# The first expert's tokens by one-hot products, the tables between its weight tiles, and the branch for excess tokens at the end

## The chip, the cores and the metric

The kernel runs on one core of one Trainium2 chip. Its engines are TensorE (PE), VectorE (DVE), ScalarE (ACT), GpSimd (POOL) and SyncE (SP); they run side by side and wait for each other by semaphores. SP, ACT and POOL also issue DMAs. The metric is the device time of one execution in microseconds (us). The kernel before takes 1837.77 us, the median of three runs (1836.67 to 1837.92).

## The reference

Two blocks work on 512 tokens of 1024 features, in float32. The first ends in a mixture of 32 experts, of which each token uses four:

```python
h      = rms_norm(x, norm_moe_w)
logits = h @ router_w + router_b              # (512, 32)
gates  = softmax(top_4(logits))               # 4 experts for each token
for e in range(32):                           # gate_up (1024, 2048), down (1024, 1024)
    g, u = split_even_odd(h_e @ gate_up[e] + b_gate_up[e])
    g, u = minimum(g, 7), clip(u, -7, 7)
    y += gate_e * (((u + 1) * g * sigmoid(1.702 * g)) @ down[e] + b_down[e])
```

This is condensed from the reference's words. After the experts come an embedding of the token (`p`, `ple_proj_w`, `ple_gate_w`) and a norm, and then the second block: a sparse attention by an indexer, a chunked causal attention, and the product with `w_out_2`.

## The kernel before

The program has three stages: `front` (norm, retention, pooling, `w_out`, router), `moe`, and `back` (embedding and attention). What moves lies in `moe` and on its two edges.

**The router's row tiles.** The 512 tokens are four row tiles of 128. `front` computes h tile by tile; the router takes each tile's top four, writes the normalised rows to `hn_d` in HBM (L667, L668) and a copy of h to `y_d` (L619), to which the experts' outputs are later added. For each token and expert, `by_e` holds the token's place among the expert's tokens and its gate.

**Experts, tiles and chunks.** An expert's weights are 12 chunks of 1 MiB, each holding two tiles of 128 rows by 1024 columns, so 384 chunks in all. Float32 precision comes from three products of rounded parts: ACT copies a tile to a rounded high part (L937), DVE subtracts that from the tile for the low part (L938), and PE multiplies. The experts are taken in the order of their load. For "many" experts (0 and the odd ones up to 29; up to 96 tokens) a tile costs six matmuls of 512 columns, in the helper `mm3`: high by x's high part (L187), high by x's low part (L188), low by x's high part (L189), first for one half of the columns and then for the other. "Few" experts (the even ones from 2 on, and 31; up to 64 tokens) have both parts of x side by side and four matmuls for a tile (L942). The bias product (L1051) stands ahead of a half's eight tiles.

**The streams and the jobs.** Two generators, `many` and `few`, yield after each tile; from the 24th tile on (`ALONE`) they take turns. Between tiles, `next_tile` runs jobs that are due: tables of tokens (`table`), an expert's gather by indirect DMA (L890) and its transposes (L905) in `fetch`, the activation (`clamped`, `folded`), and the scaled output that POOL adds to `y_d` by indirect DMA (`out`, L1028). Their place in the program, on every in-order engine, is thus fixed by the count of tiles. The two PSUM banks of the jobs are lent out by `bank`.

**The ring.** Weight chunks arrive in 7 slots: two of the pool `wr`, three of `wr2`, and two halves of the tile h, which is free once h has been copied out. An eighth early chunk goes to `ys`, the buffer of outputs. SP issues the loads in order (L167; L1167 for the early ones); each waits until its slot's tiles have been split.

**The start of the experts.** In a row and ahead of the first tile stand: the gates and the table of expert 0, its gather, the split of the gate-up biases (`bt`, L1162), `arrange` (ranks the experts by load, writes their order, `beyond` and, by L799 to L805, all tables' input), the early loads, `overflow`, and the transposes of expert 0's gathered tokens. `overflow` is a branch, `tc.If(most > 0)` at L1080: were an expert to hold more tokens than its tile, the rest would be worked there. Its condition is the number `beyond`, computed from the data; here it is zero, so the branch isn't taken. On the untaken side each engine waits for its own work, SP for all loads that it and ACT have issued, POOL for all of its own DMAs, and POOL then counts those up on SP's behalf.

**The end.** `gated_bias` adds the gates times the experts' down biases; it starts at expert 11. After the last tile `back` loads p (`pt`, L1215), `ple_proj_w` (`wp`, L1217) and the sums (`h<-y_d`, L1265), multiplies `pt` by `wp`, and sums squares of h (L251).

Of the kernel before, what the change touches and what calls it, by code (L numbers as in the profile page):

```python
# [19 lines left out]
D = 1024  # L20
NE = 32
# [14 lines left out]
ALONE, LAG = 24, 5  # L36
# [106 lines left out]
class Kern:  # L143
# [189 lines left out]
    def run(self):  # L333
        tc, nc, I = self.tc, self.nc, self.I
        with ExitStack() as g:
# [8 lines left out]
            with ExitStack() as a:  # L344
                wr2 = a.enter_context(tc.tile_pool(name="wr2", bufs=3))
                self.wr = [wr2, wr, wr2, wr, wr2]
                self.wh = [wh] * 2
                self.rp = a.enter_context(tc.tile_pool(name="rp", bufs=1))
                self.junk = self.rp.tile([128, D], BF16, name="junk")
                with ExitStack() as f:  # L350
                    self.front(f)
                with ExitStack() as f:
                    Q = f.enter_context(tc.tile_pool(name="mq", bufs=2, reuse_waits="tile"))
                    self.wr = [wr, wr2, wr, wr2, wr2] + [Part(self.h[:, 2 * i:2 * i + 2, :]) for i in range(2)]
                    self.moe(f, Q)
                self.wr, self.wh = [wr], [wh]
# [303 lines left out]
    def router(self, t, hT, s2, hg, T):  # L660
# [99 lines left out]
    def arrange(self, P, T, sel):  # L760

        nc, c = self.nc, self.c
        cp = self.tr.tile([128, 512], F32, tag="tr", name="tr")
# [6 lines left out]
        nc.vector.scalar_tensor_tensor(out=key, in0=cp[:, 0:NE], scalar=float(NE), in1=c["key"], op0=ALU.mult, op1=ALU.add)  # L770
        nc.vector.tensor_tensor(out=own, in0=key, in1=c["sel"], op=ALU.mult)
# [10 lines left out]
        kp = self.tr.tile([128, 512], F32, tag="tr", name="tr")  # L782
        nc.tensor.matmul(kp[:, 0:NE], rank[0:NE, 0:1].to_broadcast([NE, 128]), perm[0:NE, 0:NE], start=True, stop=True)
        ki = P.tile([128, NE], I32, name="ki")
        nc.vector.tensor_copy(ki, kp[:, 0:NE])
        self.order = P.tile([128, NE], I32, name="order")
# [10 lines left out]
        tp = self.tr.tile([128, 512], F32, tag="tr", name="tr")  # L797
        for t in range(NT):
            nc.tensor.transpose(tp[0:64, self.tok(t)], self.by_e[:, t].rearrange("p a e -> p (a e)"), c["ident"])  # L799
        bt = T.tile([128, S], F32, tag="ag", name="by_t")[0:64]  # L800
        nc.scalar.activation(bt, tp[0:64, :], AF.Copy)
        bp = self.tr.tile([128, NT, 2, NE], F32, tag="tr", name="tr")
        for t in range(NT):
            nc.tensor.matmul(bp[:, t].rearrange("p a e -> p (a e)"), bt[:, self.tok(t)], perm, start=True, stop=True)
        nc.vector.tensor_copy(self.by_i, bp)  # L805
        self.gates(self.by_i[:, :, 1], self.tcols, NE, T)

    def moe(self, f, Q):
# [18 lines left out]
        xgs = [P.tile([CAP, D], F32, name=f"xg{i}") for i in range(2)]  # L827
# [44 lines left out]

        def tables(e, t3):
            for j in range(BATCHES[e]):
                tabs[e + j] = [a[:, j:j + 1] for a in t3]

        def table(e):

            ps, free = yield from bank()
# [44 lines left out]
        def chunks(src, ps, pair, raw=(), bias=None, few=False):  # L924


            if bias is not None and not few:
                for n in range(2):
                    bias(n, True)
            for c0 in range(0, 8, 2):  # L930
                w = raw.pop(0) if raw else self.load(src(c0 * 128, 256).rearrange("o (k p) n -> p (o k) n", p=128), 2, 1024)
                for kk in range(2):
                    k = c0 + kk
                    hi, lo = self.next(parts)
                    if raw:
                        nc.vector.tensor_copy(hi[:, 0:1], tabs[0][1])
# [180 lines left out]
        def gated_bias():  # L1117

            bd = T.tile([128, D], F32, tag="yb", name="bd", bufs=1)
            for r in range(0, 128, NE):  # L1120
                nc.sync.dma_start(bd[r:r + NE], I["expert_b_down"][0])
            bs = P.tile([128, D], F32R, name="bs")
            yield 8
            nc.scalar.activation(bs, bd, AF.Copy)
            nc.vector.tensor_tensor(out=bs[64:128], in0=bd[64:128], in1=bs[64:128].bitcast(F32), op=ALU.subtract)
            rows = P.tile([128, NT], I32, name="rows")
            for t in range(NT):
                g4 = T.tile([128, 4, NE], F32, tag="g4", name="g4", bufs=1)
                nc.vector.tensor_copy(g4, self.G[:, t, None, :].to_broadcast([128, 4, NE]))
                nc.vector.tensor_scalar(rows[:, t:t + 1], c["far"], 128.0 * t - FAR - 1, None, op0=ALU.add)  # L1130
                yield 1
                tp, free = yield from bank()
                nc.tensor.transpose(tp[:, 0:128], g4.rearrange("p a e -> p (a e)"), c["ident"])
                yield LAG
                gT = T.tile([128, 128], F32R, tag="gT", name="gT", bufs=1)
                nc.scalar.activation(gT, tp[:, 0:128], AF.Copy)
                yield 1
                for r in (32, 96):
                    q = slice(r, r + NE)
                    nc.vector.tensor_tensor(out=gT[q], in0=tp[q, 0:128], in1=gT[q].bitcast(F32), op=ALU.subtract)  # L1140
                free()
                yield 1
                y = T.tile([128, D], F32, tag="yb", name="yb", bufs=1)
                for n in range(2):
                    ps, free = yield from bank()
                    nc.tensor.matmul(ps, gT, bs[:, n * 512:n * 512 + 512], start=True, stop=True)
                    yield LAG
# [4 lines left out]
                yield 8  # L1152
# [5 lines left out]
        nc.vector.tensor_copy(bt[:, 0:1], tabs[0][1])  # L1158
        nc.scalar.activation(bt, braw, AF.Copy)
        for r in (32, 96):  # L1160
            q = slice(r, r + NE)
            nc.vector.tensor_tensor(out=bt[q], in0=braw[q], in1=bt[q].bitcast(F32), op=ALU.subtract)  # L1162
        self.arrange(P, T, sel)
# [6 lines left out]
        raws = [early(i, self.next(self.wr).tile([128, 2, 1024], F32, tag="wr", name="wr")) for i in range(7)]  # L1170
        overflow()
        raws.append(early(7, ys))

        def stream(es):

            for e, after in zip(es, es[1:] + [None]):
# [5 lines left out]
                if e == 11:  # L1182
                    job(gated_bias())
# [19 lines left out]
        while self.jobs:  # L1203
            next_tile()

# [478 lines left out]
```

## Time and profile before

| | |
|---|---|
| median of 3 runs | 1837.77 us |
| profiled execution | 1836.86 us |
| its span | 1835.0 us |
| mean granted TensorE clock | 0.981 |
| PE busy | 1739.8 us (95%) |
| PE weight loads busy | 1285.0 us (70%) |
| DVE busy | 1529.2 us (83%) |
| ACT busy | 1193.9 us (65%) |
| POOL busy | 221.2 us (12%) |
| HBM read | 470.90 MB |

The rows are read from the one profiled execution, whose times run from the start of its span; what lies around the span is 1836.86 - 1835.0 = 1.86 us. Busy shares are means over stages that differ: the router's last tile ends near 222 us, the experts' weights stream until about 1363 us, and the rest is `back`. A releaser behind an arrow is the event that ended an idle time last. A tile's name without a number stands for all of its buffers.

### The profile page before, as it was taken

The numbers are of one execution on the slowest core, as the hardware profiler recorded it, in microseconds if no ns is written. First come the engines' busy times: TensorE is split into PE (matmuls) and PEld (weight loads), VectorE is DVE, ScalarE is ACT, GpSimd is POOL, SyncE is SP. The second block draws the span as 40 slices with busy tenths as digits, with TensorE's granted clock in tenths as the row PEclk, the third lists the DMA queues.
The fourth block names the chain that finished last, engine by engine and source line by source line (L and its number), as shares of the span: only waits on it lengthen the run. The fifth ranks groups of instructions, "written<-read, shape, count | busy, mean of one in ns | idle before, by whom it ended". The sixth has DMA issues, their size and how long they took to land. (4 is left out here: it accounts for less than half of the span.)

```text
span 1835.0 us, 24671 instructions
## 1 busy us (share of the span) xinstructions
PE 1739.8 (95%) x8375; PEld 1285.0 (70%) x8379; DVE 1529.2 (83%) x2665; ACT 1193.9 (65%) x1591; POOL 221.2 (12%) x124
## 2 busy tenths in 40 slices
PE   8999779999999998999999999999978999999999
PEld 6887657666776775766666666766656777787776
DVE  5574589999999998999999999999977769999542
ACT  5224258778878777887788788788875445554431
POOL 0011212131111311210201211110310000000000
PEclk9999879999999998999999999999999999999999
DMA  8224469999999999999999999999985222201211
GB/s 283 85 95 149 147 219 354 384 354 389 378 391 386 373 379 363 341 391 383 379 374 393 384 371 395 383 382 391 391 291 188 91 63 82 89 28 53 84 54 40
DMA packets 148295, 493.18 MB, mean 269 GB/s; under 512 B 14369, under 2 KB 18721, under 8 KB 148160
## 3 DMA queue, kind: packets, MB, share of 16 engines
q1 hardware_dynamic: 137600, 462.02, 67.1%
q0 software_dynamic: 8640, 24.78, 6.0%
q10 hardware_dynamic: 1920, 4.72, 0.7%
q8 instruction: 68, 1.11, 0.2%
q14 instruction: 67, 0.55, 0.1%
HBM read 470.90 MB, written 25.17 MB: 270 GB/s over the span
## 5 line engine op out<-in xcount | busy, mean ns | idle before, releaser
L938 DVE TENSOR_TENSOR wl<-wr,wh 128x1024 fp32r<-128x1024 f32 x550 | 641.8, 1215 | 30.9 <-ACT wh L937 30.1
L937 ACT ACTIVATE wh<-wr 128x1024 fp32r<-128x1024 f32 x550 | 544.1, 1050 | 46.3 <-DMA wr<-in_expert_w_gate_up_dram 19.0
L938 DVE TENSOR_TENSOR wl<-h,wh 128x1024 fp32r<-128x1024 f32 x216 | 252.9, 1215 | 13.8 <-ACT wh L937 13.8
L189 PE MATMUL mm<-wl,x 128*96 128x512 f32 x512 | 208.6, 407 | 16.9 <-DVE wl L938 15.9
L937 ACT ACTIVATE wh<-h 128x1024 fp32r<-128x1024 f32 x216 | 214.9, 1050 | 14.6 <-DMA h<-in_expert_w_gate_up_dram 7.3
L187 PE MATMUL mm<-wh,x 128*96 128x512 f32 x512 | 206.0, 402 | 0.7 <-ACT x L239 0.4
L188 PE MATMUL mm<-wh,x 128*96 128x512 f32 x512 | 203.2, 397 | 0.0
L1028 POOL DMA_INDIRECT y_d<-ys,gi x48 | 116.9, 2435 | 640.5 <-ACT ys L1026 390.8
L942 PE MATMUL mm<-wl,x 128*128 128x512 f32 x512 | 169.8, 412 | 1.4 <-DVE wl L938 1.2
L942 PE MATMUL mm<-wh,x 128*128 128x512 f32 x512 | 168.1, 399 | 3.1 <-ACT wh L937 3.1
L189 PEld LDWEIGHTS mm<-wl,x 128*96 128x96 f32 x512 | 82.9, 162 | 72.5 <-DVE wl L938 41.1
L189 PE MATMUL mm<-wl,a 128*96 128x512 f32 x256 | 103.9, 406 | 15.1 <-DVE wl L938 15.0
L942 PEld LDWEIGHTS mm<-wh,x 128*128 128x128 f32 x512 | 96.2, 189 | 31.2 <-ACT wh L937 4.0
L187 PE MATMUL mm<-wh,x2h 128*128 128x512 f32 (+2 forms) x288 | 114.6, 398 | 0.3 <-ACT x2h L239 0.3
L188 PE MATMUL mm<-wh,x2l 128*128 128x512 f32 (+2 forms) x288 | 111.3, 387 | 0.0
L189 PE MATMUL mm<-wl,x2h 128*128 128x512 f32 (+2 forms) x288 | 111.0, 387 | 0.1
L942 PEld LDWEIGHTS mm<-wl,x 128*128 128x128 f32 x512 | 89.0, 189 | 29.7 <-DVE wl L938 13.2
L181 DVE TENSOR_TENSOR wl<-wr,wh 128x2048 fp32r<-128x2048 f32 (+3 forms) x40 | 76.6, 1915 | 36.7 <-ACT wh L180 36.5
L188 PEld LDWEIGHTS mm<-wh,x 128*96 128x96 f32 x512 | 83.6, 163 | 33.3 <-DVE x L241 0.4
L187 PEld LDWEIGHTS mm<-wh,x 128*96 128x96 f32 x512 | 83.2, 163 | 31.3 <-ACT wh L937 3.5
L890 POOL DMA_INDIRECT xg<-hn_d,gi x32 | 67.6, 2114 | 291.4 <-PE tr L905 229.5
L187 PE MATMUL mm<-wh,a 128*96 128x512 f32 x256 | 102.2, 399 | 0.0
(437 smaller groups left out, 3271.2 us busy)
## 6 DMA issues: line engine op xcount, KB each, us to landing
wr<-in_expert_w_gate_up_dram SPq DMA_DIRECT2D x184, 1024.0 KB, 12.6
wr<-in_expert_w_down_dram SPq DMA_DIRECT2D x91, 1024.0 KB, 13.0
h<-in_expert_w_gate_up_dram SPq DMA_DIRECT2D x71, 1024.0 KB, 11.9
h<-in_expert_w_down_dram SPq DMA_DIRECT2D x37, 1024.0 KB, 13.5
wr<-in_w_in_dram SPq DMA_DIRECT2D x20, 1024.0 KB, 5.1
wr<-in_w_out_dram SPq DMA_DIRECT2D x8, 1024.0 KB, 4.9
wr<-in_ple_gate_w_dram SPq DMA_DIRECT2D x4, 1024.0 KB, 5.3
wr<-in_w_in_dram SPq DMA_DIRECT2D x4, 512.0 KB, 5.6
```

What stands on the lines that cost most here:

```text
L181: nc.vector.tensor_tensor(out=lo[:, sl], in0=raw[:, sl], in1=hi[:, sl].bitcast(F32), op=ALU.subtract)
L187: mm(out, a[0], b[0], start=first, stop=False)
L188: mm(out, a[1], b[0], start=False, stop=False)
L189: mm(out, a[0], b[1], start=False, stop=last)
L890: nc.gpsimd.indirect_dma_start(out=xgs[LESS[e]][0:m], out_offset=None, in_=self.hn_d[:, :], in_offset=bass.IndirectOffsetOnAxis(ap=tabs[e] ...
L937: nc.scalar.activation(hi, w[:, kk], AF.Copy)
L938: nc.vector.tensor_tensor(out=lo, in0=w[:, kk], in1=hi.bitcast(F32), op=ALU.subtract)
L942: nc.tensor.matmul(ps[:, n, :], pair[2][:, k, :], part[:, n * 512:n * 512 + 512], start=k == 0 and part is hi, stop=k == 7 and part is lo)
L1028: nc.gpsimd.indirect_dma_start(out=self.y_d[:, :], out_offset=bass.IndirectOffsetOnAxis(ap=rows[0:m // n], axis=0), in_=y[o:o + m // n], i ...
```

## The change

Line numbers have grown in the changed file: L938 becomes L952, L942 L956, L905 L922, L1051 L1068, L1028 L1045, L1080 L1097, L1215 L1251.

1. Expert 0's tokens are no longer gathered. Four comparisons build `first`, a one-hot matrix of tokens by places, from `by_e`; 32 float32 matmuls (L1182) multiply the rows of h by it, straight into the transposed form that L922 would give. For that the router writes the normalised rows over h in SBUF, and `hn_d` is copied from there. The two loads into h's halves come after these matmuls.
2. The bias split, the gates, the tables of the next experts and `arrange` become one job, `startup`, whose pieces stand between the first tiles.
3. For many experts a tile's matmuls run in another order: both halves of the columns by high and high, both by high and low, then both of the low part. The bias product moves to the eighth tile.
4. The ring gets an eighth slot (pool `wr4`); the ninth early chunk goes to `ys`.
5. `overflow` moves behind the last tile, and `gated_bias` to expert 29, the last of the many. Its buffers change.
6. `ALONE` goes from 24 to 32.

```diff
-ALONE, LAG = 24, 5
+ALONE, LAG = 32, 5
...
-                    self.wr = [wr, wr2, wr, wr2, wr2] + [Part(self.h[:, 2 * i:2 * i + 2, :]) for i in range(2)]
+                    more = f.enter_context(tc.tile_pool(name="wr4", bufs=1, reuse_waits="tile"))
+                    self.wr = [wr, wr2, wr, wr2, wr2, more] + [Part(self.h[:, 2 * i:2 * i + 2, :]) for i in range(2)]
...
-            nc.scalar.activation(hg[j], hg[j], AF.Copy, scale=rs)
-            nc.scalar.dma_start(self.hn_d[self.tok(t), 512 * j:512 * j + 512], hg[j])
+            o = slice(512 * j, 512 * j + 512)
+            nc.scalar.activation(self.h[:, t, o], hg[j], AF.Copy, scale=rs)
+            nc.scalar.dma_start(self.hn_d[self.tok(t), o], self.h[:, t, o])
...
-            if bias is not None and not few:
-                for n in range(2):
-                    bias(n, True)
...
-                        nc.vector.tensor_copy(hi[:, 0:1], tabs[0][1])
+                        nc.vector.tensor_copy(hi[:, 0:1], first[:, NT - 1, 0:1])
...
-                        for n in range(2):
-                            nn = slice(n * 512, n * 512 + 512)
-                            self.mm3(ps[:, n, :], (pair[0][:, k, :], pair[1][:, k, :]), (hi[:, nn], lo[:, nn]),
-                                     bias is None and k == 0, k == 7)
+                        if bias is not None and k == 7:
+                            for n in range(2):
+                                bias(n, False)
+                        for x, part in ((pair[0], hi), (pair[1], hi), (pair[0], lo)):
+                            for n in range(2):
+                                nc.tensor.matmul(ps[:, n, :], x[:, k, :], part[:, n * 512:n * 512 + 512],
+                                                 start=k == 0 and x is pair[0] and part is hi, stop=k == 7 and part is lo)
...
-        self.gates(self.G[:, :, 0:2], self.tcols0, 2, T)
-        tables(0, self.slots(0, BATCHES[0], Q))
-        gather(0)
...
-        self.arrange(P, T, sel)
+        first = P.tile([128, NT, CAP], F32, name="first")
+        for t in range(NT):
+            nc.vector.tensor_scalar(first[:, t], c["iota"][:, 0:CAP], self.by_e[:, t, 0, 0:1], None, op0=ALU.is_equal)
+        X[0] = pair(CAP, "x")
+        xp = self.mm.tile([128, 2, 512], F32, tag="mm", name="mm")
+        for t in range(NT):
+            for k in range(8):
+                nc.tensor.matmul(xp[:, k // 4, k % 4 * CAP:k % 4 * CAP + CAP], self.h[:, t, k * 128:k * 128 + 128], first[:, t],
+                                 start=t == 0 and k % 4 == 0, stop=t == NT - 1 and k % 4 == 3)
+        for j in range(2):
+            self.split_in(xp[:, j, 0:4 * CAP].rearrange("p (n m) -> p n m", n=4), [a[:, 4 * j:4 * j + 4] for a in X[0][0:2]], slice(0, CAP))
+
+        def startup():
+
+            order = self.arrange(P, T, sel, bank)
+            next(order)
+            yield 1
+            nc.scalar.activation(bt, braw, AF.Copy)
+            for r in (32, 96):
+                q = slice(r, r + NE)
+                nc.vector.tensor_tensor(out=bt[q], in0=braw[q], in1=bt[q].bitcast(F32), op=ALU.subtract)
+                yield 1
+            raws.append(early(8, ys))
+            self.gates(self.G[:, :, 0:2], self.tcols0, 2, T)
+            yield from table(0)
+            yield from order
+            ready.append(True)
+            yield from table(2)
...
-        raws = [early(i, self.next(self.wr).tile([128, 2, 1024], F32, tag="wr", name="wr")) for i in range(7)]
-        overflow()
-        raws.append(early(7, ys))
+        raws = [early(i, self.next(self.wr).tile([128, 2, 1024], F32, tag="wr", name="wr")) for i in range(8)]
...
-                if e == 11:
-                    job(gated_bias())
+                if not LESS[e] and after is None:
+                    job(gated_bias(), 2)
...
-        X[0] = pair(CAP, "x")
-        now(turned(xgs[0], CAP, X[0]))
         J[0, "x"] = None
-        job(table(2))
-        J[2, "x"] = job(fetch(2, 6))
+        job(startup())
+        J[2, "x"] = job(fetch(2, 8))
...
         while self.jobs:
             next_tile()
+        overflow()
```

The next rows are PE's instructions at the end of the router and the start of the experts, in the changed kernel. L702 is the router's last matmul, `first` the one-hot matrix, L767 the sums for the ranking in `arrange`.

```order
L702 MATMUL tr<-mask,b_before 128x32 [waits DVE_49]
L1182 MATMUL mm<-first,h 128x96 [waits DMAHW6_49,DMAHW4_49,DVE_49]
L1182 MATMUL mm<-first,h 128x96 x23
L1182 MATMUL mm<-first,h 128x96 [waits DVE_49,Activation_49]
L1182 MATMUL mm<-first,h 128x96 x3
L1182 MATMUL mm<-first,h 128x96 [waits Activation_49]
L1182 MATMUL mm<-first,h 128x96 x3
L767 LDWEIGHTS b_ones
L767 MATMUL tr<-mask,b_ones 128x32
```

Before, the sums and the tables followed the router's last matmul, then came the branch, the transposes and the bias; now the one-hot products come first, and the sums stand behind them.

On DVE of the changed kernel this follows `by_e` of the last row tile (L705). `wh` and `wl` are a tile's high and low part, `key` (L772) is the ranking's first step, `x` the split of expert 0's tokens, `bt` the bias split.

```order
L952 TENSOR_TENSOR wl<-wr,wh 128x1024 [waits DMAHW7_49,Activation_49]
L772 SCALAR_TENSOR_TENSOR key<-tr,c_small 128x32 [waits PE_49]
L952 TENSOR_TENSOR wl<-wr,wh 128x1024 [waits Activation_49]
L241 TENSOR_TENSOR x<-mm,x 128x4x96 [waits Activation_49]
L774 TENSOR_TENSOR own<-key,c_small 128x32 [waits DVE_49]
L1195 TENSOR_TENSOR bt<-ys,bt 32x1024 [waits DMAHW6_49,Activation_49]
L241 TENSOR_TENSOR x<-mm,x 128x4x96 [waits Activation_49]
L775 TENSOR_REDUCE rank<-own 128x1 [waits DVE_49]
L1195 TENSOR_TENSOR bt<-ys,bt 32x1024 [waits DMAHW2_49]
L776 TENSOR_SCALAR own<-key,rank 128x32 [waits DVE_49]
```

The ranking stood in one piece ahead of the first subtraction; now its steps lie between subtractions, and `key` waits on PE.

On SP these rows, of the kernel before, follow the last load of expert weights; `wr<-in_ple_gate_w` are weights of `back`.

```order
L167 DMA wr<-in_ple_gate_w_dram 128x4x512 [waits DMAHW3_49,DVE_49]
L167 DMA wr<-in_ple_gate_w_dram 128x4x512 [waits DMAHW5_49,DMAHW1_49,DVE_49]
L1215 DMA pt<-in_p_dram 128x4x256 [waits DMAHW6_49,DMAHW2_49,DVE_49]
L1217 DMA wp<-in_ple_proj_w_dram 128x2x1024 [waits DMAHW4_49]
L1265 DMA h<-y_d 128x1024 [waits DMASW5_49]
```

And these of the changed kernel, from the end of the branch's body on; L1097 closes its untaken side.

```order
L1097 UNCONDITIONAL_BRANCH [waits SP_sequencer_49,DMAHW0_49,DMAHW1_49,DMAHW2_49,DMAHW3_49,DMAHW4_49,DMAHW5_49,DMAHW6_49,DMAHW7_49]
L1251 DMA pt<-in_p_dram 128x4x256 [waits DMAHW4_49,DMAHW2_49,DVE_49]
L1253 DMA wp<-in_ple_proj_w_dram 128x2x1024 [waits DMAHW3_49]
L1301 DMA h<-y_d 128x1024 [waits DMASW6_49,DMASW4_49,DMAHW4_49,DMASW2_49,DMAHW7_49,DMASW0_49,DVE_49]
L1301 DMA h<-y_d 128x1024 [waits DMAHW5_49,DVE_49]
```

The two loads of `ple_gate_w` stay ahead of the branch; the loads of `pt`, `wp` and `h<-y_d` come behind it.

## Rows read from the trace of the kernel before

**Rows 1.** Windows, all engines: stretch, its length, busy time, clock, DMA share, GB/s.
```profile
222.00:230.00 8.00, 2.71 (x19) 1.54 (x18) 5.71 (x35) 0.99 (x3) 0.00 (x0) 0.50 0.69 232
230.00:241.00 11.00, 1.93 (x8) 1.77 (x8) 9.95 (x29) 6.74 (x7) 1.06 (x1) 0.50 0.15 42
241.00:251.00 10.00, 7.87 (x33) 4.67 (x33) 5.84 (x25) 2.16 (x3) 0.99 (x1) 0.50 0.51 154
251.00:282.00 31.00, 30.79 (x153) 21.09 (x153) 29.63 (x60) 24.88 (x30) 7.22 (x3) 1.00 0.98 332
300.00:1355.00 1055.00, 1014.01 (x4700) 719.98 (x4699) 986.07 (x1173) 841.95 (x978) 176.51 (x75) 1.00 1.02 379
```

**Rows 2.** Timeline of PE, 222 to 246 us: start, length, instruction, [idle before, releaser].
```profile
222.19 0.19 PE L700 MATMUL tr<-mask,b_before 128*128 128x32 bf16 x1 [3.80 <-DVE mask L693]
...
230.22 1.93 PE L804 MATMUL tr<-perm,by_t 64*128 64x64 f32 x8 [0.43 <-DMA bd<-in_expert_b_down_dram]
242.71 1.51 PE L905 MATMUL tr<-c_lasting,xg 96*128 96x96 f32 x8 [10.56 <-DVEq L1080]
...
245.50 0.74 PE L187 MATMUL mm<-wh,x 128*96 128x512 f32 x1 [0.42 <-ACT x L239]
```

**Rows 3.** Timeline of SP's DMA issues, 240 to 251 us.
```profile
240.41 0.39 SPq L167 DMA_DIRECT2D wr<-in_expert_w_gate_up_dram  x1
250.15 0.39 SPq L1167 DMA_DIRECT2D ys<-in_expert_w_gate_up_dram  x1
```

**Rows 4.** Timeline of DVE, at the branch and at 274 us.
```profile
242.89 0.58 DVE L741 TENSOR_SCALAR oh<-b_iota,by_i 128x128 bf16<-128x128 bf16 x3 [1.91 <-DVEq L1080]
...
274.57 2.34 DVE L938 TENSOR_TENSOR wl<-wr,wh 128x1024 fp32r<-128x1024 f32 x2
```

**Rows 5.** Timeline of PE in the pooling, 130 us.
```profile
130.51 0.38 PE L570 MATMUL tr<-band,h 128*128 128x128 f32 x2
130.73 0.39 PE L569 MATMUL tr<-band,h 128*128 128x128 f32 x2
```

**Rows 6.** Timeline of ACT, the router's last tile.
```profile
216.75 0.34 ACTq L619 DMA_DIRECT2D y_d<-h  x1
...
220.27 1.34 ACT L667 ACTIVATE hg<-hg,rsy 128x512 f32<-128x512 f32 x2 [2.43 <-issue]
```

**Rows 7.** The page's costliest groups: busy, mean ns, idle before, and its main releaser.
```profile
L938 DVE TENSOR_TENSOR wl<-wr,wh 128x1024 fp32r<-128x1024 f32 x550 | 641.8, 1215 | 30.9 <-ACT wh L937 30.1
L937 ACT ACTIVATE wh<-wr 128x1024 fp32r<-128x1024 f32 x550 | 544.1, 1050 | 46.3 <-DMA wr<-in_expert_w_gate_up_dram 19.0
...
L189 PE MATMUL mm<-wl,x 128*96 128x512 f32 x512 | 208.6, 407 | 16.9 <-DVE wl L938 15.9
```

**Rows 8.** Timeline of PE, the end of the experts and the start of `back`.
```profile
1362.77 0.73 PE L942 MATMUL mm<-wl,a 128*128 128x512 f32 x2
...
1373.22 0.79 PE L187 MATMUL mm<-wph,php 128*128 128x512 f32 x1 [3.71 <-ACT wph L1252]
...
1385.46 0.79 PE L187 MATMUL mm<-wph,php 128*128 128x512 f32 x1 [5.95 <-ACT pp L1646]
...
1390.74 0.50 PE L187 MATMUL mm<-wph,php 128*128 128x512 f32 x1
```

**Rows 9.** Timeline of SP's DMA issues, the same stretch.
```profile
1352.92 5.66 SPq L167 DMA_DIRECT2D wr<-in_ple_gate_w_dram  x2
1360.47 0.37 SPq L1215 DMA_DIRECT2D pt<-in_p_dram  x1
...
1380.49 1.77 SPq L1265 DMA_DIRECT2D h<-y_d  x4
```

**Rows 10.** Timeline of ACT, the same stretch.
```profile
1383.77 1.06 ACT L251 ACTIVATE junk<-h 128x1024 bf16<-128x1024 f32 x1 [10.32 <-DMA h<-y_d]
```

**Rows 11.** Timeline of POOL, the last scatter.
```profile
1375.96 1.41 POOL L1028 DMA_INDIRECT y_d<-ys,gi  x1 [3.33 <-DMA y_d<-ys,gi]
```

**Rows 12.** The page's DMA issues: count, size, us to landing.
```profile
wr<-in_ple_gate_w_dram SPq DMA_DIRECT2D x4, 1024.0 KB, 5.3
```

More of the change, by code (lines that the diff above doesn't have):

```diff
@@ L758, in slots_by, with arrange @@
         yield gi, gt
-    def arrange(self, P, T, sel):
+    def arrange(self, P, T, sel, bank):
         nc, c = self.nc, self.c
-        cp = self.tr.tile([128, 512], F32, tag="tr", name="tr")
+        cp, free = yield from bank()
         for t in range(NT):
@@ L780, in arrange @@
         nc.vector.tensor_scalar(perm, c["ranks"][0:64], rank[0:64, 2:3], None, op0=ALU.is_equal)
-        kp = self.tr.tile([128, 512], F32, tag="tr", name="tr")
+        kp, free = yield from bank()
         nc.tensor.matmul(kp[:, 0:NE], rank[0:NE, 0:1].to_broadcast([NE, 128]), perm[0:NE, 0:NE], start=True, stop=True)
+        yield 2
         ki = P.tile([128, NE], I32, name="ki")
         nc.vector.tensor_copy(ki, kp[:, 0:NE])
+        free()
         self.order = P.tile([128, NE], I32, name="order")
@@ L795, in arrange @@
         nc.vector.tensor_copy(self.beyond, cf)
-        tp = self.tr.tile([128, 512], F32, tag="tr", name="tr")
+        tp, free = yield from bank()
         for t in range(NT):
             nc.tensor.transpose(tp[0:64, self.tok(t)], self.by_e[:, t].rearrange("p a e -> p (a e)"), c["ident"])
+        yield 2
         bt = T.tile([128, S], F32, tag="ag", name="by_t")[0:64]
         nc.scalar.activation(bt, tp[0:64, :], AF.Copy)
-        bp = self.tr.tile([128, NT, 2, NE], F32, tag="tr", name="tr")
+        free()
+        yield 1
+        bp, free = yield from bank()
+        bp = bp[:, 0:2 * NT * NE].rearrange("p (t a e) -> p t a e", t=NT, a=2)
         for t in range(NT):
             nc.tensor.matmul(bp[:, t].rearrange("p a e -> p (a e)"), bt[:, self.tok(t)], perm, start=True, stop=True)
+        yield 2
         nc.vector.tensor_copy(self.by_i, bp)
+        free()
         self.gates(self.by_i[:, :, 1], self.tcols, NE, T)
@@ L826, in moe @@
             nc.scalar.dma_start(braw[r:r + NE], I["expert_b_gate_up"][0][:, r // 64 * D:r // 64 * D + D])
-        xgs = [P.tile([CAP, D], F32, name=f"xg{i}") for i in range(2)]
+        xgs = [P.tile([128, D], F32, name=f"xg{i}") for i in range(2)]
         for x in xgs:
@@ L871, in now @@
                 pass
+        ready = []
         def tables(e, t3):
@@ L877, in table @@
         def table(e):
+            while e and not ready:
+                yield 1
             ps, free = yield from bank()
@@ L1117, in gated_bias @@
         def gated_bias():
-            bd = T.tile([128, D], F32, tag="yb", name="bd", bufs=1)
+            y = xgs[0]
+            bs = T.tile([128, 1536], F32R, tag=f"x{CAP}", name="bs")
+            gT, bs = bs[:, D:1536], bs[:, 0:D]
             for r in range(0, 128, NE):
[L1121 to L1125, printed above, removed]
+                nc.sync.dma_start(y[r:r + NE], I["expert_b_down"][0])
@@ L1126, in gated_bias @@
             rows = P.tile([128, NT], I32, name="rows")
             for t in range(NT):
-                g4 = T.tile([128, 4, NE], F32, tag="g4", name="g4", bufs=1)
+                nc.vector.tensor_scalar(rows[:, t:t + 1], c["far"], 128.0 * t - FAR - 1, None, op0=ALU.add)
+            tp, free = yield from bank()
+            for t in range(NT):
+                g4 = T.tile([128, 4, NE], F32, tag="g4", name="g4")
                 nc.vector.tensor_copy(g4, self.G[:, t, None, :].to_broadcast([128, 4, NE]))
-                nc.vector.tensor_scalar(rows[:, t:t + 1], c["far"], 128.0 * t - FAR - 1, None, op0=ALU.add)
@@ L1131, in gated_bias @@
                 yield 1
[L1132 to L1140, printed above, removed]
@@ L1141, in gated_bias @@
-                free()
-                yield 1
-                y = T.tile([128, D], F32, tag="yb", name="yb", bufs=1)
+                nc.tensor.transpose(tp[:, self.tok(t)], g4.rearrange("p a e -> p (a e)"), c["ident"])
+            yield LAG
+            nc.scalar.activation(gT, tp, AF.Copy)
+            nc.scalar.activation(bs, y, AF.Copy)
+            yield 1
+            for r in (32, 96):
+                q = slice(r, r + NE)
+                nc.vector.tensor_tensor(out=gT[q], in0=tp[q], in1=gT[q].bitcast(F32), op=ALU.subtract)
@@ L1144, in gated_bias @@
+            free()
+            yield 1
+            nc.vector.tensor_tensor(out=bs[64:128], in0=y[64:128], in1=bs[64:128].bitcast(F32), op=ALU.subtract)
+            yield 1
+            for t in range(NT):
                 for n in range(2):
                     ps, free = yield from bank()
-                    nc.tensor.matmul(ps, gT, bs[:, n * 512:n * 512 + 512], start=True, stop=True)
-                    yield LAG
+                    nc.tensor.matmul(ps, gT[:, self.tok(t)], bs[:, n * 512:n * 512 + 512], start=True, stop=True)
+                    yield 3
```

14 lines of the change are left out of this document (8 added, 6 removed).

## The prediction

> **What bounds the kernel now.** I read the windows first. From 300 to 1355 us [rows 1] PE is busy for 1014.0 of 1055 us, DVE for 986.1 and the 16 DMA engines all the time: in the stream of expert weights three things lie within 7% of each other, so no change to one of them alone brings much there. The stretch ahead of it is another matter. From 222 to 251 us PE works 2.71 + 1.93 + 7.87 = 12.5 of 29 us at a granted clock of 0.50, and from 230 to 251 us the DMA queues are at 0.15 and 0.51. From 251 us on all three are busy again.
>
> The order of PE's instructions [rows 2] shows what PE waits for: its last work on the tables starts at 230.22 us, the transposes of the gathered tokens only at 242.71 us, after 10.56 us of idle time put down to the branch L1080, and the first matmul of expert 0 at 245.50 us. SP [rows 3] issues one weight load at 240.41 us and the next at 250.15 us: behind the branch, whose untaken side waits on SP until that load has landed. DVE [rows 4] loses less there: 1.91 us. Of the 60 us from 222 to 282 it is busy for 5.71 + 9.95 + 5.84 + 29.63 = 51.1 us [rows 1], so 8.9 us are the most that it can gain by then if it keeps all its work.
>
> **The first expert's tokens.** Out go the gather, 8 transposes (1.51 us) and the wait before them [rows 2]. In come four comparisons on DVE and 32 matmuls L1182 of 96 columns in float32 (the order counts them as 24, 4 and 4). The nearest row is the pooling's 128-column float32 matmul L569/L570 [rows 5]: one shows as two records, and the next follows 0.22 us later at full clock. So 32 x 0.22 = 7.0 us at full clock, 14.1 us at half. The first can start when by_e of the last row tile is there; the matmul before that sum starts at 222.19 us [rows 2], so about 222.7 us. The clock is at half then [rows 1]. In the back part the same engine, after an idle gap, starts at 1385.46 us and is at full pace from 1390.74 us [rows 8]: 12 matmuls in 5.28 us, 0.44 us each. Taken over: 12 matmuls at half (5.3 us), 20 at full (4.4 us), the end at 232.4 us; bounds 229.7 and 236.8 us.
>
> [...]
>
> Then the split of x: two copies on ACT and two subtractions on DVE, as before. Expert 0 starts near 235 us in place of 245.50: PE gains 10.5 us at this point.
>
> **What DVE makes of it.** The ranking, the tables and the bias split have not gone; the changed order puts them between the subtractions L952 (L938 before) of the first weight tiles. By that order DVE does `first`, one subtraction, and then `key`, which waits for the sums L767, and these stand behind all 32 matmuls L1182 on PE. DVE therefore has little to do from about 227 to 233 us: about 6.4 us of the 8.9 are idle again, and 2.5 us is its lead at 282 us. DMA gains more: with the branch gone, loads can follow as slots come free. Eight early loads plus ys fill one slot more, though the two into h must now wait for L1182 (about 232 us) where nothing held them back. Before, 8 chunks of 1 MiB are in by 250 us, and 31 us at 332 GB/s less the gathers bring some 8 more by 282 us: 16. Now 9 are loaded early, and each two subtractions free a slot; DVE's 21st ends at 276.9 us before [rows 4], so near 274.4 us now: 10 slots, of which 9.5 loads may have landed by 282 us, 9 + 9.5 = 18.5 chunks. The difference of 2.5 chunks is 7 us at the 379 GB/s of the stream [rows 1].
>
> Which lead reaches the end of the stream? DVE waits 30.9 us for ACT's copies of ring chunks and ACT in turn 19.0 us for those loads [rows 7]; a lead in DMA removes such waits until it is used up, a lead in DVE persists. I put the gain at the end of the stream between 2.5 (DVE's lead only) and 10.5 us (PE's lead, all others following) and take 6.5, nearest to DMA's 7.
>
> **Other edits in the stream.** Low products last: L189 waits 16.9 us for the low part in one group [rows 7]; the low part may now come two matmuls later. But DVE, which delivers it, is no faster, so most of it turns into another wait: 0, bounds 0 and -8. The eighth slot lengthens the queue but not the pace of a DMA that is busy all the time: 0, bounds +2 and -5. The first bias product behind seven tiles, and few starting after 32 tiles in place of 24, move work inside the stream: 0, bounds -3 and +3. gated_bias keeps its matmuls and four scatters; its last scatter stands 30 tiles before the end, ahead of the final ones: 0 to +1. Writing the normalised rows over h needs the copy y_d<-h to be done: it is issued at 216.75 us, and the multiplication starts at 220.27 us [rows 6]; 0, at most +2.
>
> **The branch at the end.** What the branch cost at 240 us it now costs behind the last weight tile. SP's order puts pt, wp and h<-y_d behind it, and its untaken side waits until the loads of ple_gate_w have landed. These are issued from 1352.92 us, the second 5.3 us on, pt at 1360.47 us [rows 9]; such a load lands in 5.3 us [rows 12], so at about 1363.5 us. At 240.41 us the same landing (about 245.7 us) left 4.5 us until SP's next load [rows 3]. So pt is issued at 1364 to 1368 us, 3.5 to 7.5 us later. The projection that needs pt and wp starts at 1373.22 us now; PE then rests 5.95 us and goes on at 1385.46 us, because ACT waits for h<-y_d, whose first use starts at 1383.77 us [rows 8, 10]. So that delay is hidden for some 6 us, and the exposed part is y_d: SP issues it at 1380.49 us, when the last scatter (1375.96 us on POOL) has landed [rows 9, 11]. Now POOL first waits for that scatter itself, then passes the branch and only then releases SP. Nothing shows this price; bounds are 0 and the 9.7 us between SP's loads in [rows 3]; I take 2.5 us, near DVE's 1.91 us in [rows 4].
>
> [...]
>
> **Sum.** -6.5 + 2.5 = -4.0 us on the profiled execution of 1836.86 us (span 1835.0 and 1.86 around it), 1832.9 us. The median, 1837.77, lies 0.9 us higher than that execution, so 1833.8, rounded 1833.5 us.
>
> **Rivals.** (a) PE's head start is kept whole: the hand-over low-last and the eighth slot let DVE and DMA follow. -10.5 - 1 + 2 = about -9.5, 1828 us; for it, DMA was idle for 14 of the 21 us from 230 to 251 us [rows 1]; against it, DVE's 8.9 us. (b) The start is DVE's, and what it gains the end takes: -2.5 + 2.5 = 0, 1838 us. For it speaks the order (`key` behind L767); against it DVE's waits on loads later on. (c) The branch at the end decides: POOL's untaken side costs as much as SP's at 240 us, h<-y_d comes 8 us later and all of the back part with it, -2.5 + 8 = +5.5, 1843 us. It decides from the point where POOL's release comes more than 6.5 us after 1380.5 us. Against it: ACT, DVE and PE pass their branches early, and most of POOL's can lie under the scatter's landing. (d) The one-hot products don't start expert 0 sooner, because the clock stays at half and h comes late: like (b), with PE at 238 us, about 1838 us.
>
> **How the numbers follow.** Forecast 0.38, (a) 0.20, (b) and (d) 0.24, (c) 0.18. From no change this kernel can be told by about 0.2%, 3.7 us: faster is below 1834.1, slower above 1841.4. The forecast lies just at the first bound, and I count two thirds of it as faster, a third as same: faster 0.25 + 0.20 + 0.03 = 0.48, same 0.13 + 0.15 = 0.28, slower 0.18 + 0.06 = 0.24. Range: down to (a) with the stream's bounds of low-last and the slot (-8, half believed), 1821 us; up to (c), 1843 us. The forecast's own range is 1830 to 1837 us.
>
> **What would show it.** In the changed profile: 32 matmuls L1182 from about 223 to 232 us, the clock back before 230 us; the first L966 near 235 us; DVE idle some 6 us before L772; SP's loads without a hole from 233 us on; the last L956 near 1357 us in place of 1362.77 [rows 8]; pt near 1361 us; h<-y_d 2.5 us later against the last scatter. The forecast is wrong if the last L956 has moved by less than 3 us or more than 9, or if h<-y_d follows the last scatter by over 8 us.

## The result and the profile after

The changed kernel takes 1856.01 us (median of 4 runs, 1854.37 to 1857.18) against 1837.22 us for the kernel before: a ratio of 1.0106, 95% interval 1.0088 to 1.0123. It is slower by 1%, 19 us, where 4 us faster was forecast and 1821 to 1843 us was the range. The profiled execution took 1857.05 us, its span 1855.3 us.

The windows of the changed kernel, in the columns of [rows 1], and a sixth one near the end of the expert weights:

```profile
222.00:230.00 8.00, 5.86 (x28) 5.68 (x27) 5.75 (x35) 3.62 (x6) 0.00 (x0) 0.50 0.30 100
230.00:241.00 11.00, 9.38 (x67) 7.56 (x66) 5.80 (x10) 5.65 (x7) 0.00 (x0) 0.95 0.73 221
241.00:251.00 10.00, 9.34 (x41) 6.18 (x42) 9.54 (x26) 5.24 (x6) 0.00 (x0) 1.00 0.96 352
251.00:282.00 31.00, 28.59 (x143) 19.17 (x142) 29.17 (x74) 21.83 (x25) 4.02 (x3) 0.94 0.79 265
300.00:1355.00 1055.00, 1003.24 (x4612) 706.96 (x4610) 966.08 (x1149) 818.38 (x954) 156.45 (x74) 0.98 1.01 374
1255.00:1340.00 85.00, 57.02 (x233) 39.47 (x231) 49.52 (x49) 46.25 (x53) 9.12 (x6) 0.82 0.85 272
```

The start went as intended: from 222 to 251 us PE works 24.6 us, before 12.5, with its clock back at full from about 231 us on (the mean from 230 to 241 us is 0.95). The last row is new. For 85 us PE is busy for 57 and DVE for 49.5, the clock is at 0.82, and even the DMA queues are not full (0.85).

To see where the two kernels part, I counted the subtractions of L938 and L952 in DVE's timeline. Each of the 768 weight tiles has one, so the end of the n-th says how far the stream of weights is:

| subtraction, counted from 0 | before, us | after, us | difference |
|---|---|---|---|
| 16 | 271.6 | 263.3 | -8.3 |
| 40 | 305.5 | 306.4 | +0.9 |
| 280 | 656.3 | 653.8 | -2.5 |
| 400 | 839.9 | 824.5 | -15.4 |
| 664 | 1221.8 | 1201.3 | -20.5 |
| 712 | 1289.6 | 1287.1 | -2.5 |
| 736 | 1322.0 | 1339.5 | +17.5 |
| 767, the last | 1362.7 | 1382.0 | +19.3 |

At tile 664 the changed kernel was 20 us ahead. Within the next 72 tiles it lost 38 us. Most of the first 20 us were won around tiles 296 to 400, where the kernel before has its `gated_bias`; the loss lies where the changed kernel has it. What waited there, from the list of waits of all engines, 1240 to 1345 us (us in total, times, longest):

```profile
DVE wl L952 <- ACT wh L951: 35.4, 7, 21.2
ACT xg L1167 <- DMA y_d<-xg,rows: 30.6, 2, 21.7
...
PE mm L966 <- ACT wh L951: 20.3, 1, 20.3
```

L1167 is ACT's copy of a bias product into `y`. DVE waits for ACT's copies of weight tiles, PE for the same, and ACT for a DMA: the scatter that still reads `y`. The timeline of ACT shows what stands behind the wait:

```profile
1265.12 0.60 ACT L1167 ACTIVATE xg<-tr 128x512 f32<-128x512 f32 x1 [8.97 <-DMA y_d<-xg,rows]
...
1297.97 7.69 ACT L951 ACTIVATE wh<-wr 128x1024 fp32r<-128x1024 f32 x8
1327.34 1.08 ACT L1167 ACTIVATE xg<-tr 128x512 f32<-128x512 f32 x2 [21.67 <-DMA y_d<-xg,rows]
```

And the timeline of POOL why the scatter is so late:

```profile
1254.26 2.13 POOL L1169 DMA_INDIRECT y_d<-xg,rows  x1 [27.29 <-ACT x L239]
1295.46 1.42 POOL L1045 DMA_INDIRECT y_d<-ys,gi  x1 [39.08 <-ACT ys L1043]
1304.36 1.75 POOL L1045 DMA_INDIRECT y_d<-ys,gi  x1 [7.48 <-DMA y_d<-ys,gi]
1312.75 1.42 POOL L1045 DMA_INDIRECT y_d<-ys,gi  x1 [6.64 <-issue]
1321.29 1.57 POOL L1169 DMA_INDIRECT y_d<-xg,rows  x1 [7.12 <-DMA y_d<-ys,gi]
```

`y` was full at 1287.6 us, but POOL first had an expert's output to wait for and then three outputs to scatter. All scatters add to the same `y_d`, and they were issued 8.4 to 8.9 us apart; for the second and the fourth the trace names the landing of the one before as what POOL waited for. The scatter of `y` was issued at 1321.29 us and landed before 1327.34 us, and only then could ACT write the next product into the only buffer. ACT's weight copies stood in its queue behind that.

The other rows that answer to those of before. PE at the start [rows 2]:

```profile
223.81 0.18 PE L702 MATMUL tr<-mask,b_before 128*128 128x32 bf16 x1 [4.75 <-DVE mask L695]
224.32 10.63 PE L1182 MATMUL mm<-first,h 128*128 128x96 f32 x64 [0.33 <-DVE by_e L705]
...
235.58 0.68 PE L966 MATMUL mm<-wh,x 128*96 128x512 f32 x2 [0.34 <-issue]
```

SP's issues [rows 3], without the hole of 9.7 us (the longest pause is 3.8 us):

```profile
231.45 3.97 SPq L1206 DMA_DIRECT2D h<-in_expert_w_gate_up_dram  x2
236.43 0.37 SPq L167 DMA_DIRECT2D wr<-in_expert_w_gate_up_dram  x1
240.61 0.37 SPq L1206 DMA_DIRECT2D ys<-in_expert_w_gate_up_dram  x1
242.81 3.16 SPq L167 DMA_DIRECT2D wr<-in_expert_w_gate_up_dram  x2
```

DVE [rows 4], whose `key` waits for PE:

```profile
228.19 1.23 DVE L952 TENSOR_TENSOR wl<-wr,wh 128x1024 fp32r<-128x1024 f32 x1 [1.46 <-ACT wh L951]
235.08 0.19 DVE L772 SCALAR_TENSOR_TENSOR key<-tr,c_small 128x32 f32<-128x32 f32 x1 [5.66 <-PE tr L767]
```

The end of the weights on PE [rows 8], then SP [rows 9], POOL [rows 11] and ACT [rows 10]:

```profile
1382.07 0.73 PE L956 MATMUL mm<-wl,a 128*128 128x512 f32 x2
...
1393.34 0.79 PE L187 MATMUL mm<-wph,php 128*128 128x512 f32 x1 [2.62 <-ACT wph L1288]
```

```profile
1366.29 6.33 SPq L167 DMA_DIRECT2D wr<-in_ple_gate_w_dram  x2
1378.49 0.38 SPq L1251 DMA_DIRECT2D pt<-in_p_dram  x1
...
1400.12 1.77 SPq L1301 DMA_DIRECT2D h<-y_d  x4
```

```profile
1393.26 1.41 POOL L1045 DMA_INDIRECT y_d<-ys,gi  x1 [3.47 <-DMA y_d<-ys,gi]
```

```profile
1403.80 1.06 ACT L251 ACTIVATE junk<-h 128x1024 bf16<-128x1024 f32 x1 [10.24 <-DMA h<-y_d]
```

`h<-y_d` comes 6.86 us after the last scatter, before 4.53: the branch costs 2.3 us there. The first use of h is 20.0 us later than before, almost as much as the last weight tile (19.3 us). ACT waits 10.24 us for `h<-y_d`, before 10.32.

### The profile page after: what moved, and what is told of

Same layout as the page of the kernel before. It is cut to its first block, busy times and chain, and to the rows that moved or that the text cites. A ratio compares the mean times of both kernels' runs of the same rounds, so it can differ in the third digit from the quotient of the medians.

```text
span 1855.3 us, 24781 instructions
## 1 busy us (share of the span) xinstructions
PE 1758.6 (95%) x8431; PEld 1293.2 (70%) x8435; DVE 1528.2 (82%) x2664; ACT 1184.6 (64%) x1587; POOL 198.9 (11%) x123
## 3 DMA queue, kind: packets, MB, share of 16 engines
q10 hardware_dynamic: 1920, 4.72, 0.7%
## 5 line engine op out<-in xcount | busy, mean ns | idle before, releaser
L952 DVE TENSOR_TENSOR wl<-wr,wh 128x1024 fp32r<-128x1024 f32 x576 | 671.8, 1217 | 45.7 <-ACT wh L951 45.7
L966 PE MATMUL mm<-wh,x 128*96 128x512 f32 x1024 | 285.4, 399 | 2.8 <-ACT gs L1016 0.9
L952 DVE TENSOR_TENSOR wl<-h,wh 128x1024 fp32r<-128x1024 f32 x190 | 224.2, 1220 | 22.8 <-ACT wh L951 22.8
L966 PEld LDWEIGHTS mm<-wh,x 128*96 128x96 f32 x1024 | 164.6, 163 | 71.2 <-ACT wh L951 1.5
L951 ACT ACTIVATE wh<-h 128x1024 fp32r<-128x1024 f32 x190 | 191.3, 1051 | 13.0 <-DVE wl L952 5.8
L956 PE MATMUL mm<-wl,x 128*128 128x512 f32 x512 | 177.7, 427 | 8.3 <-DVE wl L952 8.0
L966 PE MATMUL mm<-wl,x 128*96 128x512 f32 x512 | 165.1, 403 | 10.8 <-DVE wl L952 10.1
L956 PE MATMUL mm<-wh,x 128*128 128x512 f32 x512 | 170.1, 403 | 1.8 <-ACT wh L951 1.6
L966 PE MATMUL mm<-wh,a 128*96 128x512 f32 x512 | 142.2, 398 | 20.3 <-ACT wh L951 20.3
L1045 POOL DMA_INDIRECT y_d<-ys,gi x48 | 80.4, 1675 | 652.1 <-ACT ys L1043 536.5
L956 PEld LDWEIGHTS mm<-wl,x 128*128 128x128 f32 x512 | 85.4, 190 | 59.8 <-DVE wl L952 46.9
L966 PEld LDWEIGHTS mm<-wh,a 128*96 128x96 f32 x512 | 82.6, 163 | 54.1 <-ACT wh L951 20.9
L956 PEld LDWEIGHTS mm<-wh,x 128*128 128x128 f32 x512 | 96.9, 190 | 29.3 <-ACT wh L951 2.8
L966 PEld LDWEIGHTS mm<-wl,x 128*96 128x96 f32 x512 | 78.7, 163 | 53.9 <-DVE wl L952 25.5
L180 ACT ACTIVATE wh<-wr 128x2048 fp32r<-128x2048 f32 (+3 forms) x40 | 64.6, 1615 | 45.4 <-PE mm L188 41.0
L956 PE MATMUL mm<-wl,a 128*128 128x512 f32 x256 | 88.0, 425 | 3.1 <-DVE wl L952 3.0
```

The costliest lines, as they stand in the source:

```text
L180: nc.scalar.activation(hi[:, sl], raw[:, sl], AF.Copy)
L951: nc.scalar.activation(hi, w[:, kk], AF.Copy)
L952: nc.vector.tensor_tensor(out=lo, in0=w[:, kk], in1=hi.bitcast(F32), op=ALU.subtract)
L956: nc.tensor.matmul(ps[:, n, :], pair[2][:, k, :], part[:, n * 512:n * 512 + 512], start=k == 0 and part is hi, stop=k == 7 and part is lo)
L966: nc.tensor.matmul(ps[:, n, :], x[:, k, :], part[:, n * 512:n * 512 + 512], start=k == 0 and x is pair[0] and part is hi, stop=k == 7 and ...
L1045: nc.gpsimd.indirect_dma_start(out=self.y_d[:, :], out_offset=bass.IndirectOffsetOnAxis(ap=rows[0:m // n], axis=0), in_=y[o:o + m // n], i ...
```

## The experiments

Two theories stood after the profile. **Theory 1:** the move of `gated_bias` to the end, with one buffer, is the loss. **Theory 2:** the end of the stream is slow for another reason (few experts alone, scatters in a row, the branch), and ACT's wait only shows it. Ratios are to the kernel before on the same chip, with 95% intervals; each profile is of one execution.

**Three buffers for the products (e1).**

```diff
+            self.wr.remove(self.more)
+            two_y = self.more.tile([128, 2, 1024], F32, tag="wr", name="wr")
+            yb = [xgs[0], two_y[:, 0], two_y[:, 1]]
...
             for t in range(NT):
+                y = yb[(t + 1) % 3]
```

> The changed kernel, but gated_bias writes its products in turn to three buffers (expert 0's x buffer and the eighth ring slot, taken out of the ring then) instead of one. Theory 1 (in the changed kernel ACT, in order, waits 9.0 and 21.7 us for a scatter of gated_bias before it may overwrite the one buffer, and the weight stream stands still behind it): both waits go, the last L956 ends 30 to 38 us earlier, near 1346 us, total 1818 to 1826 us. Theory 2 (the stream is slow at its end for another reason: few experts alone, seven scatters in a row, and the wait only shows it): at most 10 us better, above 1845 us.

Measured: 1830.55 us, ratio 0.9979 (0.9966 to 0.9992). The two waits are gone, and with them the sign of the result: now it is 0.2% faster than before. From tile 664 to tile 736 the stream takes 105.9 us, with one buffer 138.2; the difference of 32.3 us is near the 30.6 us of the two waits. The last subtraction ends at 1352.9 us, 29.1 us earlier. Total and last tile both improve by less than theory 1 expected, and the total lies outside its range: at tiles 664 to 712 8.1 us of the lead still go. In that stretch its window reads

```profile
1220.00:1240.00 20.00, 18.56 (x69) 13.33 (x70) 14.61 (x14) 15.19 (x17) 2.10 (x1) 0.83 0.98 339
```

with DVE at 14.6 of 20 us and PE's clock at 0.83 on average.

**The changed kernel without gated_bias (e2), the kernel before without it (e3).** In e2 the line `job(gated_bias(), 2)` becomes `pass`, in e3 `job(gated_bias())`.

> The changed kernel without gated_bias: the gates times the experts' down biases are left out. Theory 1: 1812 to 1822 us, somewhat below the three buffers, since its 8 matmuls, 4 scatters and copies go too. Theory 2: above 1840 us.

> The kernel before without gated_bias (the gates times the down biases left out). If the 9 us that the changed kernel gains between tiles 296 and 312 come from the place of gated_bias at expert 11 (ACT waits 4.3 us for its scatter there): 1820 to 1830 us. If they come from the order of products or the eighth slot: 1833 to 1837 us.

Measured: e2 1817.17 us, ratio 0.9912 (0.9885 to 0.9939); e3 1819.59 us, ratio 0.9921 (0.9895 to 0.9947). e2 came as theory 1 had it; e3 lies 0.4 us below the range that put the gain at the place of gated_bias, on the far side from the other one. Together they split the result. By the spans of the profiles, gated_bias costs 1835.0 - 1818.1 = 16.9 us in the kernel before and 1855.3 - 1815.5 = 39.8 us in the changed one: 22.9 us more. All other edits together are 1815.5 - 1818.1 = -2.6 us. The sum is the 20.3 us between the two profiles. By the ratios, which rest on more executions, the two costs are 14.5 and 35.6 us, 21 us apart, and the other edits are -1.7 us. Each interval reaches 3 to 5 us to either side, so the other edits together can't be told from nothing.

**The kernel before with only gated_bias moved, in its new form (e4).**

```diff
-                if e == 11:
-                    job(gated_bias())
+                if not LESS[e] and after is None:
+                    job(gated_bias(), 2)
```

> The kernel before with only gated_bias in its new form, one buffer, and at expert 29. Theory 1: the same stall comes at the end, 20 to 36 us against some 10 us that go at expert 11: 1850 to 1868 us. Theory 2: 1826 to 1840 us.

Measured: 1852.41 us, ratio 1.0098 (1.0072 to 1.0124), within theory 1's range. The one buffer is here a tile of its own, `yb`. The same wait stands in the list of waits from 1230 to 1345 us:

```profile
ACT yb L1150 <- DMA y_d<-yb,rows: 25.5, 3, 14.7
```

This one edit alone gives nearly the whole loss (1.0106). Theory 2 falls: neither the branch nor the streams' lengths are changed here.

**e1 without the scatters of gated_bias (e5).** The `indirect_dma_start` in its loop is left out.

> e1 (three buffers) with everything of gated_bias but its four scatters: the products are formed and never added. e1 still costs 13.4 us more than e2, which has no gated_bias. If that is the traffic and the queue of the scatters (each reads and writes 0.5 MB in a stream in which the DMA engines are always busy, and POOL's next scatters stand behind them): near e2, 1817 to 1822 us. If it is the work of the job on the in-order engines: near e1, 1826 to 1831 us.

Measured: 1824.65 us, ratio 0.9945 (0.9926 to 0.9964), between the two expectations. At tile 712 e5 lies 8.1 us behind e2, as e1 does (9.2); the job's work on the in-order engines costs that, or the ring slot that both give up for the buffers; no run separates these two. At the last tile e5 is 8.3 us behind and e1 13.3: the scatters cost 5 us more.

**The down biases in the part behind the experts (e6, e9).** The job only turns the gates and sends them to HBM; behind the experts come, for each row tile,

```diff
+            for n in range(2):
+                nn = slice(512 * n, 512 * n + 512)
+                ps = self.mm.tile([128, 512], F32, tag="mm", name="mm")
+                nc.tensor.matmul(ps, gT[0:NE, self.tok(t)], bd[0:NE, nn], start=True, stop=True)
+                nc.vector.tensor_tensor(out=ht[:, nn], in0=ht[:, nn], in1=ps, op=ALU.add)
```

in e6 behind the whole projection, in e9 for the first row tile between the projection's second and third.

> The changed kernel without the gated_bias job: the transposed gates go through HBM, and the part behind the experts multiplies them by the down biases (8 float32 matmuls of 512 columns, where PE rests 6 us in the kernel before) and adds them to h on DVE. Theory 1 (the place of gated_bias in the stream, its single buffer and its scatters are the whole loss): e2 plus 2 to 6 us for the additions ahead of the norm, 1819 to 1824 us, faster than both kernels. If the branch at the end or the start were the loss, above 1835 us.

> e6, but the first row tile's two bias products stand on PE between the second and the third row tile of the embedding's projection, and no longer behind all of it. In e6 the last weight tile ended as early as in e2, but the first sum of squares started 14.5 us later, since the additions to h stood behind the whole projection. If that order was the 9 us that e6 has over e2: 1817 to 1822 us. If the float32 products and additions themselves cost it: within 2 us of e6, 1824 to 1828 us.

Measured: e6 1826.22 us, ratio 0.9961 (0.9940 to 0.9981), a miss upwards: its last tile ended as in e2 (1339.7 us), but the first sum of squares came at 1378.29 us, in e2 at 1363.82. e9, with the order mended: 1821.87 us, ratio 0.9922 (0.9905 to 0.9940), just inside the range that its expectation gave to the order. The two rows, of e6 and of e9:

```profile
1378.29 1.04 ACT L251 ACTIVATE junk<-h 128x1024 bf16<-128x1024 f32 x1
```

```profile
1368.88 1.06 ACT L251 ACTIVATE junk<-h 128x1024 bf16<-128x1024 f32 x1 [3.49 <-DVE h L1291]
```

e9 is the fastest version with all of the reference's work, 0.8% faster than the kernel before.

**The old order of the products (e7), seven ring slots (e10), ALONE at 24 (e11), each on e1.** e7 calls `mm3` for each half again, e10 leaves `more` out of the ring, e11 sets `ALONE` back.

> e1 with the old order of a many tile's six products (for each half of the columns high-high, high-low, low-high). If low products last gain anything: 1 to 8 us slower than e1, 1832 to 1838 us; as the prediction priced it (0): within 2 us of e1, 1829 to 1832 us.

> e1 with seven ring slots for the whole stream, the eighth used for the two buffers alone, and ys for the eighth early chunk. As the prediction priced the slot (0, bounds +2 and -5): within 2 us of e1, near 1830 us. If the slot carries the gain in the stream: 1833 to 1838 us, and the last weight tile 3 to 8 us later than in e1.

> e1 with the few experts' stream from the 24th tile on, as before, and not from the 32nd. As priced (0, bounds -3 and +3): within 3 us of e1, 1828 to 1833 us.

Measured: e7 1828.76 us, ratio 0.9968 (0.9951 to 0.9986); e10 1834.00 us, 0.9993 (0.9981 to 1.0004); e11 1832.44 us, 0.9986 (0.9973 to 0.9999). All three intervals overlap with e1's (0.9966 to 0.9992). The order of products and ALONE are worth nothing that can be told in the total; e7, on another chip than e1, came out 0.2 us below the range for an order that gains nothing, and 3 us from the other. e10 lies where its expectation put a slot that carries a gain: 1834.00 us, and its last subtraction ends at 1356.7 us, 3.8 us after e1's. By the ratios the slot is worth 2.6 us, inside the prediction's bounds; the overlap leaves it unsettled.

**The kernel before with only the branch at the end (e8).** `overflow()` moves behind the last `next_tile()`.

> The kernel before with only the branch moved behind the last tile. The prediction's terms: at the start SP's hole of 9.7 us between loads and PE's 10.56 us of idle time shrink (gain of 2 to 7 us at tile 40), at the end h<-y_d comes 2 to 2.5 us later against the last scatter: 1830 to 1836 us. A branch at the end that costs as much as the hole at the start (rival c): 1838 us or more.

Measured: 1832.43 us, ratio 0.9981 (0.9961 to 1.0000). In its profile the stream is 2.8 us ahead of the kernel before at tile 40 and 6.5 us at the last tile, and the end gives 2.1 us of it back: `h<-y_d` 6.65 us after the last scatter. The total, the gain at tile 40 and the price at the end are as expected. But 3.9 of the 6.5 us are won between tiles 296 and 312, in the stall at gated_bias, and not at the branch's old place. POOL's and SP's rows of e8:

```profile
1369.57 1.41 POOL L1028 DMA_INDIRECT y_d<-ys,gi  x1 [6.26 <-DMA y_d<-ys,gi]
```

```profile
1376.22 1.77 SPq L1265 DMA_DIRECT2D h<-y_d  x4
```

The same distance is 6.58 in e1, 6.59 in e2, 6.61 in e5 and 6.86 us in the changed kernel (7.00 and 7.38 in e6 and e9), and 4.53, 4.55 and 4.37 in the three with the branch at the start (before, e3, e4). Rival (c), with 8 us at this place, falls.

## Why the prediction was wrong

**The step that failed** is the sentence "gated_bias keeps its matmuls and four scatters; its last scatter stands 30 tiles before the end, ahead of the final ones: 0 to +1." It counted work and looked at the last scatter. It did not ask what the next product waits for: each is written into the one buffer `y`, and that is free only when POOL has issued the scatter before and it has landed. Measured, the term is +22.9 us by the spans and +21 by the ratios (e2 and e3 against their kernels), and e4 shows it by itself. With it the last L956 came at 1382.07 us, where the prediction's own sign of being right was 1357. The loss does not lie in the later place as such: there the job costs 13.4 us with three buffers (medians of e1 and e2), at expert 11 15.4 (the kernel before and e3). Two changes met at the one buffer, and no run separates them. The products follow each other after 3 and 5 tiles where it was 5 and 8 and more for the transposes, and the job ran into the stretch in which the last many experts' outputs queue on POOL. The wait is dear because ACT, which waits, also makes the high part of every weight tile, for which DVE waits 35.4 us and PE 20.3 from 1240 to 1345 us. The kernel before had the same hazard in small: in its list of ACT's waits from 590 to 860 us stands

```profile
ACT yb L1148 <- DMA y_d<-yb,rows: 4.3, 1, 4.3
```

The prediction made no use of it, since it costed that edit at nothing.

**That gated_bias was dear where it stood** was missed as well. It costs 16.9 us by the spans (14.5 by the ratios) in the kernel before, for 4 scatters, 8 matmuls and some copies. No rival had this, so none could put the time above 1843 us.

**The start** went nearly by the steps. L1182 was to run from 222.7 to 232.4 us and ran from 224.32 to 234.8. It began 1.6 us late because the router's sum did. Some 1 us of that belongs to the change: the sum waits 4.72 to 4.75 us for `mask` in the nine profiles with the new start, 3.58 to 3.81 in the four with the old. L1182 took 10.5 us in place of 9.7: the clock was to be back by 228 us and stood at 0.50 to about 231, with PE busy all the time from 226 us on. From 232 us to the end of L1182 it was 1.00, and not at half. The first L966 was to come near 235 us and came at 235.58. DVE's idle time before `key` was to be 6.4 us and is 5.66, with 1.46 before the first subtraction. Its lead at 282 us was to be 2.5 us; at tile 24 (282.9 us) it is 1.3, and at tile 40 nothing is left. The 2.5 chunks of lead in DMA did not come: its share is 0.79 from 251 to 282 us, since DVE, busy with the tables then, freed no slots: in that stretch SP waits 18.3 us for DVE's subtractions, and issues no load from 262.3 to 274.36 us.

**The stream.** The forecast was 6.5 us. Without gated_bias on either side the last subtraction ends 1347.5 - 1339.6 = 7.9 us earlier, so the size fits. The way there does not: the gain was to be a lead from the start. These are the ends of the subtractions at tile 40 and at tile 664, ahead of the late gated_bias's stall:

| profiles | tile 40, us | tile 664, us |
|---|---|---|
| changed kernel, e1, e2, e5, e6, e9 | 304.8 to 306.4 | 1199.5 to 1201.3 |
| e11 (`ALONE` at 24) | 304.0 | 1201.7 |
| e7 (old order of products) | 306.9 | 1202.3 |
| e10 (seven slots) | 304.7 | 1203.6 |
| e4, e3 (old start and stream, no gated_bias at expert 11) | 306.5, 310.0 | 1205.8, 1206.6 |
| e8, before (gated_bias at expert 11) | 302.7, 305.5 | 1215.4, 1221.8 |

At tile 40 the one-hot products have won nothing against the kernel before and e4, and e8, with the branch alone moved, is the earliest of all. Up to there e3 lacks only gated_bias's first steps, mainly the loads of the down biases, which SP issues from 227.86 us on, long before expert 11; so the start can differ by some 4 us for no more than that. Nor does such a lead last: e4 is 3.6 us ahead of e3 at tile 40 and 0.8 at tile 664. The changed stream's lead over these two is 4.5 to 7.1 us at tile 664, and the three runs with one edit of the stream undone lie 1.0 to 2.9 us behind e1 (1200.7 us), though only e10 by more than the six profiles differ among themselves. So the lead seems to come from the slot, the order and `ALONE`, which were priced at 0 with bounds down to -8, -5 and -3, and not from the branch's hole or the one-hot products. This rests on one profile of each and is not shown beyond that; no run had the products alone.

**The branch at the end** was priced at 2.5 us and costs 2.1 to 2.3 us between the last scatter and `h<-y_d`. That `pt` comes later is hidden, as forecast. The branch instructions are a small part of it. In the changed kernel's trace `COMPARE_BRANCH` (L1097) takes 0.05 to 0.07 us on SP, ACT, POOL and DVE; on PE, which does not stand between the scatter and `h<-y_d`, it lasts 5.18 us. After the landing, from 1397.95 us on, POOL's `INC_SWDGE_SEM`, the counting up on SP's behalf, takes 2.01 us (at the old place, in the kernel before, 0.38), and `h<-y_d` is issued 0.16 us after its end.

The 4.5 us that the prediction read between the landing and SP's next load, and by which it put `pt` at up to 1368 us, are a weak ground. In the kernel before SP's next load came 4.1 us after the landing (246.01 us by its semaphore), but in e3, with the same branch at the same place, 0.8 us after it (246.20 and 247.04 us), and in e8, with the branch at the end, `pt` followed 0.6 us after it (1359.24 and 1359.80 us), in the changed kernel 0.8 us (1377.72 and 1378.49 us).

**The sum of the terms without that one** was -4 us (the last step, 1833.8 rounded to 1833.5, is a slip of no weight); e2 against e3 gives -2.6 us by the spans and -1.7 by the ratios. These runs do not contradict the forecast of the rest, but they don't show its sign either, and since the stream's lead, as far as these profiles tell, did not come from where it was forecast, that the size fits is luck.

## What to carry to other kernels

When a job is moved, follow each of its buffers: who frees it, on which queue that stands, and what that queue holds at the new place. A wait on an in-order engine costs what else that engine serves, here the whole stream of weights (30.6 us of ACT's waits, and 32.3 us less from tile 664 to 736 without them), so a copy that may wait for a DMA should have more than one buffer (three in e1) or stand on an engine with nothing behind it (no run tried that). Before pricing a move at nothing, price the thing where it stands now: leaving it out of both kernels takes two runs and showed 17 and 40 us here.

## What the runs showed that was not expected

Scatters that add to the same tensor ran one after the other: in the changed kernel POOL issues three at 1295.46, 1304.36 and 1312.75 us, though ACT had written what they read by 1298.1 us; for the second the record names the landing of the first as what it waited for, for the third it names nothing. While ACT waited, PE ran dry and its clock fell too: it was 0.82 on average from 1255 to 1340 us, and 0.50 from 1315 to 1327 us, where PE did nothing. ACT's wait ended at 1327.34 us, but the clock was still 0.50 up to 1333 us and 1.00 only from 1334 us on, so that a part of what followed the stall ran at half speed as well. Two L966 matmuls of a tile's low part took 1.06 us from 1331.24 us and 0.62 us from 1333.74 us; the windows before and after:

```profile
1327.00:1333.00 6.00, 3.58 (x9) 2.39 (x10) 3.60 (x4) 5.66 (x7) 1.57 (x1) 0.50 0.40 53
1334.00:1340.00 6.00, 6.00 (x33) 4.77 (x31) 4.04 (x5) 3.83 (x5) 0.00 (x0) 1.00 0.97 298
```
